# A third seven-product chunk per eight, with one weight sum formed by an accumulating load

## The chip, the cores and the metric

The kernel runs on one core of one Trainium2 chip. The metric is the device time of one execution in microseconds (us), as the median of several runs. In the text PE is TensorE, DVE is VectorE, ACT is ScalarE, POOL is GpSimd and SP is SyncE, as in the profile.

## The reference

One encoder layer on a sequence of 256 tokens of width 2048, in float32, and a final norm. What is computed:

```
x = x + 1/2 * SwiGLU_1(RMSNorm(x))        # w_gate, w_up: 2048 x 5632, w_down: 5632 x 2048
h = RMSNorm(x)
u, v, g = split(h @ w_in)                 # w_in: 2048 x 7168
x = x + (sigmoid(g_a) * PoolBranch(u) + sigmoid(g_b) * ConvBranch(v)) @ w_out
x = x + 1/2 * SwiGLU_2(RMSNorm(x))
out = RMSNorm(x)
SwiGLU(h) = (silu(h @ w_gate) * (h @ w_up)) @ w_down
```

Nearly all of the arithmetic is in the products with weights, and most of that in the two SwiGLU blocks (called FFN below). The change touches these two blocks alone; the part between them, called the mixer, stays as it is.

## The kernel before

**Precision.** Every product is formed from two-part operands: a number w is split into a high part `wh` (a cast on ACT) and a low part `wl` = w - wh (a subtraction on DVE), and x·w is xh·wh + xh·wl + xl·wh. So each block of a product costs three matmuls, and each weight that is loaded costs one ACT cast and one DVE subtraction (`hi_lo`).

**Units and chunks.** The weights come as a stream of chunks. A chunk is two rows of blocks, each a 128 x 1024 tile of 512 KB: `r0` holds blocks w11 (left half) and w12 (right half), `r1` holds w21 and w22. The tokens form two halves of 128 as well, so a chunk is a 2 x 2 by 2 x 2 block product. Normally this takes eight block products, 24 matmuls of 128x512. A unit is a run of chunks that adds into one set of accumulators in PSUM: a *gate unit* (512 hidden columns of gate and of up: 8 chunks, c0 to c7 below) or a *down unit* (1024 output columns; 8 chunks). An FFN has eleven gate units, numbered 0 to 10, and down units in pairs after gate units 4 and 8 and at the end. Gate unit 0 and the last pair take all products in the plain way; the ten other gate units and four down units of each FFN, 28 units in all, are *seven units*.

**Seven products.** In the chunks of a seven unit that `SEVEN` names (before: c0 and c3), a Strassen-Winograd form takes seven block products, 21 matmuls. It needs three sums of weight blocks, formed by four DVE additions (`split_seven`): S1 = w12 + w11, S1 + w22, w12 + w22 and S1 + w22 + w21. Three of them are split together (`exth`, `extl`, 128x1536), S1 takes w12's place in `r0`. It also needs four differences of the left operand, the *E forms* (`e_forms`: four DVE differences, an ACT cast, a DVE subtraction). For the gate products they are made once per FFN, for the down products whenever a hidden block is put in place. Four of the seven products go to PSUM banks 0 to 3 and are spread over the accumulators by `shared_parts` (one ACT copy, four DVE operations), the three others go straight to the accumulators in banks 4 to 7.

**Order.** Nothing is scheduled automatically: each engine executes its instructions in the order in which they are written, and waits where an operand is missing. `run` goes through the stream; at step i it issues the loads of chunk i+2, then the split of chunk i+1, then what stands in the table `side` for step i (`at`), then the products of chunk i. Work put into `middle` (`amid`) is written between the two halves of a plain chunk's matmuls. At the end of a gate unit (`gate_done_seven`) DVE adds the PSUM accumulators to the shared parts (two additions of 128x1024, one for each half of the tokens), ACT takes silu and DVE the product, giving the hidden tile h; the next unit's products into banks 4 to 7 wait for those two additions. h is transposed on PE one unit later by `put`, twice (k0 = 0 and 2): four transposes, an ACT cast, a DVE subtraction, and where the block belongs to a seven chunk an ACT copy `hy` and the E forms. The tiles `wh` and `wl` have four buffers each, two chunks' worth, so DVE and ACT run at most one chunk ahead of PE.

Of the kernel before, what the change touches and what calls it, by code (L numbers as in the profile page):

```python
# [8 lines left out]
F32 = mybir.dt.float32  # L9
# [29 lines left out]
TAPS_BUSY = 4  # L39

GROUP = 4
SEVEN = (0, 3)

B_P1, B_P5, B_P6, B_P7, B_11, B_12, B_21, B_22 = range(8)

# [36 lines left out]
def encoder_kernel(ctx: ExitStack, tc: tile.TileContext, x, xT, vecs, rows, pool_m,  # L82
# [30 lines left out]
    def at(i, fn):  # L113

        side.setdefault(i, []).append(fn)
# [19 lines left out]
    def raw_tile(name):  # L135
        return wraw.tile([P, W2], F32, tag="raw", name=name)

    def load(i):
        if i >= len(stream):
            return  # L140
        u, cc = stream[i]
        raw[i] = []
        for kk in range(2):
            r = raw_tile(f"raw{i}_{kk}")
            for c in range(0, W2, C if i == 0 else W2):
                s = slice(c, c + (C if i == 0 else W2))
# [3 lines left out]
            raw[i].append(r)  # L150

    def hi_lo(src, h, l=None):
        nc.scalar.copy(out=h, in_=src)  # L153
# [32 lines left out]

    def split_seven(i, r0, r1):

        w11, w12, w21, w22 = r0[:, :C], r0[:, C:], r1[:, :C], r1[:, C:]
        sm = ffn["pool"].tile([P, 3, C], F32, tag="sum", name=f"sum{i}")  # L190

        def add(out, a, b):
            nc.vector.tensor_tensor(out=out, in0=a, in1=b, op=ALU.add)  # L193
# [100 lines left out]

        return [tuple(block(pool, f"h{s}{u}", F32R, f"{name}{s}{u}") for s in "hl") for u in range(GROUP)]

    def e_tiles(pool, tag, n):

        return {c: tuple(pool.tile([P, 4, P], F32R, tag=f"{tag}E{x}{c}", name=f"{tag}E{x}{c}_{n}") for x in "hl")
                for c in SEVEN}  # L300

    def e_forms(dst, even, odd):

        e = stg.tile([P, 4, P], F32, tag="sg", name=f"e{Pos.now}")
        a11, a21, a12, a22 = even[:, :P], even[:, P:], odd[:, :P], odd[:, P:]
        for n, (a, b) in enumerate(((a11, a21), (a21, a22), (a11, e[:, 1, :]), (a12, e[:, 2, :]))):
            nc.vector.tensor_tensor(out=e[:, n, :], in0=a, in1=b, op=ALU.subtract)  # L307
        hi_lo(e, *dst)
# [8 lines left out]

    def scaled_forms(dst, src, gain_base, k0):

        y = stg.tile([P, 2, T], F32, tag="sg", name=f"y{Pos.now}_{k0}")  # L320
# [49 lines left out]
    def open_ffn(stack, n):  # L370

        pool = ffn["pool"] = stack.enter_context(tc.tile_pool(name=f"ffn{n}", bufs=1))
        ffn["ht"] = hidden(pool, f"ht{n}")
        ffn["hE"] = e_tiles(pool, "h", n)
        ffn["t0"], ffn["t1"] = (pool.tile([P, 2, C], F32, tag=f"part{t}", name=f"part{n}_{t}") for t in range(NT))

    def ffn_units(w_g, w_d, xt, xE, rs, residual_done, tail=None):
        waiting = []

        def hidden_lhs(k, t):  # L380
            return tuple(h[:, k % 4, t * P:(t + 1) * P] for h in ffn["ht"][k // 4])

        def put(u, hs, k0, b=None):
            b = transposes(lambda j, t: hs[t][:, (k0 + j) * P:(k0 + j + 1) * P], 2, f"hT{Pos.now}_{k0}", b)
            hi_lo(b.rearrange("p (q t) -> p q t", q=2), *(h[:, k0:k0 + 2, :] for h in ffn["ht"][u % GROUP]))
            c = (u % GROUP) * 2 + k0 // 2
            if c in SEVEN:
                y = stg.tile([P, 2, T], F32, tag="sg", name=f"hy{Pos.now}_{k0}")
                nc.scalar.copy(out=y, in_=b.rearrange("p (q t) -> p q t", q=2))
# [92 lines left out]
        for u in range(units):  # L482
            if u:
                add_unit(Unit(w_g[u], KD, lhs_of(xt), gate_done_seven(u), forms=forms_of(lhs_of(xt), xE),
                              early=gate_early, seven=SEVEN, start=(lambda: None) if u == 1 else None))
            else:
                add_unit(Unit(w_g[u], KD, lhs_of(xt), gate_done(u)))
# [13 lines left out]


    xt1 = pair(xtp, "x", KD, "xt1")
    xE1 = e_tiles(xtp, "x", 1)

    def start():
        nc.vector.memset(ones, 1.0)
# [11 lines left out]

    def load_x(t):  # L520
        nc.sync.dma_start(out=X[t], in_=x[t * P:(t + 1) * P, :])
        at(5, lambda: squares(t, 0, 0, D))
        if t == NT - 1:
            at(5, lambda: finish_rstd(rstd[0]))
# [12 lines left out]


    ht_stack = ExitStack()
    open_ffn(ht_stack, 1)  # L540
    xt2 = pair(xtp, "x", KD, "xt2")
    ffn_units(w_g1, w_d1, xt1, xE1, rstd[0], next_operand(xt2, V_NM, rstd[1]))
    n1 = len(stream)
# [263 lines left out]
    def wo_done(half):  # L807
        def done(acc):
            if half == 0:
                xt3.extend(pair(xtp, "x", KD, "xt3"))  # L810
                xE3.update(e_tiles(xtp, "x", 3))
# [65 lines left out]
    at(n3 - 1, final_first_half)  # L877


    xr = [block(ffn["pool"], f"xr{j}", F32, f"xr{j}") for j in range(4)]  # L880
    start()
    for i in range(PF - 1):
        load(i)
# [9 lines left out]
        at(2 + t, lambda t=t: load_x(t))  # L893
    at(KD // 2, lambda: nc.gpsimd.dma_start(out=vec[:, KD:], in_=vecs[:, KD:]))
    for c in SEVEN:
        at(c + 3, lambda c=c: scaled_forms(xE1[c], [xr[c // 2][:, 2 * c % 4 + j, :] for j in range(2)], V_N1, 2 * c))
    run(0, n1)
    ht_stack.close()

# [14 lines left out]

    ht_stack = ExitStack()
    open_ffn(ht_stack, 2)
    run(n2, n3)
    for i in sorted(side):
        for fn in side[i]:
# [88 lines left out]
```

## Time and profile before

| | |
|---|---|
| median of 3 runs | 1958.94 us (1958.81 to 1959.25) |
| the profiled execution | 1958.93 us, its span 1957.1 us |
| PE busy | 1933.4 us, 99% of the span |
| DVE busy | 1521.7 us, 78% (80 to 85% in most of the FFNs) |
| ACT busy | 979.2 us, 50% |
| POOL busy | 11.0 us |
| loads on SP's queue | 378.45 MB, 58.7% of the 16 DMA engines' time |
| granted PE clock | 0.998 |

The span of the profiled execution lies 1.8 us under its device time; that execution and the median agree. In a timeline row the first number is the start in us from the beginning of the span, the second the time in us from the start of the first instruction of the row to the end of the last; "x4" means that four instructions were merged. A bracket tells how long the engine sat idle before the row, and who ended that. A wait on another engine's result shows as idle time in front of the waiting instruction. Matmuls overlap, so their own duration (0.39 us) is longer than the distance from one to the next.

### The profile page before, as it was taken

To read this page: it belongs to the slowest core of one execution; us is meant where nothing else is said; L and a number is where in the kernel's file an instruction comes from. 1 tells how busy PE (TensorE), PEld (TensorE's weight loads), DVE (VectorE), ACT (ScalarE), POOL (GpSimd) and SP (SyncE) were. 2 spreads that over 40 slices of the span, in tenths; PEclk is the share of its full clock that TensorE was granted. 3 is DMA by queue.
4 is the path that set the end of the run, shared out by engine and by line. 5 is a ranking of instruction groups with operands and counts; after the bars stand their busy time and mean duration, and the time that the engine had idled before them with its cause. 6 is when DMAs were issued, how large, how long until landed. Compare 5 with 4: busy or idle time off the path is not lost.

```text
span 1957.1 us, 23246 instructions
## 1 busy us (share of the span) xinstructions
PE 1933.4 (99%) x8680; PEld 1598.3 (82%) x8680; DVE 1521.7 (78%) x1762; ACT 979.2 (50%) x1117; POOL 11.0 (1%) x22
## 2 busy tenths in 40 slices
PE   9999999999999999999999999999999999999998
PEld 7788888878888888888888887887888887888886
DVE  6888888888888655888898766588887888888865
ACT  6545544555445455454444545455554455455544
POOL 0000000000000000000000000000000000000000
PEclk9999999999999999999999999999999999999999
DMA  8555666555565556656666555555656565556654
GB/s 314 178 180 191 205 205 203 194 184 191 187 212 190 197 187 200 193 195 213 201 207 199 191 183 180 185 187 179 203 194 214 195 194 182 193 196 203 196 193 149
DMA packets 106145, 383.90 MB, mean 196 GB/s; under 512 B 11920, under 2 KB 12176, under 8 KB 105776
## 3 DMA queue, kind: packets, MB, share of 16 engines
q1 hardware_dynamic: 104688, 378.45, 58.7%
q0 software_dynamic: 1056, 3.83, 0.6%
q8 instruction: 68, 1.11, 0.2%
q14 instruction: 45, 0.37, 0.1%
q10 hardware_dynamic: 288, 0.14, 0.0%
HBM read 380.28 MB, written 2.10 MB: 195 GB/s over the span
## 4 chain that ended last, share of the span: by engine, by line
PE 94%; DVE 3%; ACT 1%; issue 1%; DMA 1%; DVEq 0%; POOLq 0%; ACTq 0%; POOL 0%
PE ps L256 78%; PE ps L277 13%; PE ps L343 1%; DVE wl L155 1%; DVE sum L193 1%; DVE part L413 0%; DVE extl L155 0%; ACT exth L153 0%; ACT wh L153 0%; DVE e L307 0%; DMA raw<-in_w_g 0%; PE ps L740 0%; ACT sq L358 0%; DMA xr<-in_xT 0%; PE ps L715 0%
## 5 line engine op out<-in xcount | busy, mean ns | idle before, releaser
L153 ACT CAST wh<-raw 128x1024 fp32r<-128x1024 f32 (+1 forms) x706 | 729.2, 1049 | 729.5 <-PE ps L256 361.6
L155 DVE TENSOR_TENSOR wl<-raw,wh 128x1024 fp32r<-128x1024 f32 (+1 forms) x706 | 846.2, 1219 | 316.4 <-ACT wh L153 312.8
L256 PE MATMUL ps<-wh,xt1h 128*128 128x512 f32 x544 | 169.9, 393 | 1.3 <-ACT wh L153 1.0
L256 PE MATMUL ps<-wh,xt3h 128*128 128x512 f32 x544 | 169.6, 393 | 0.0
L256 PE MATMUL ps<-wl,xt1h 128*128 128x512 f32 x544 | 168.3, 390 | 0.4 <-DVE wl L155 0.3
L256 PE MATMUL ps<-wl,xt3h 128*128 128x512 f32 x544 | 168.1, 390 | 0.3 <-DVE wl L155 0.3
L256 PE MATMUL ps<-wh,xt1l 128*128 128x512 f32 x544 | 167.7, 389 | 0.1
L256 PE MATMUL ps<-wh,xt3l 128*128 128x512 f32 x544 | 167.6, 389 | 0.0
L256 PE MATMUL ps<-wh,xt2h 128*128 128x512 f32 x448 | 138.5, 390 | 0.0
L256 PE MATMUL ps<-wh,xt2l 128*128 128x512 f32 x448 | 138.0, 389 | 0.0
L256 PE MATMUL ps<-wl,xt2h 128*128 128x512 f32 x448 | 137.9, 389 | 0.0
L256 PEld LDWEIGHTS ps<-wl,xt1h 128*128 128x128 f32 x544 | 101.9, 188 | 22.9 <-DVE wl L155 1.6
L256 PEld LDWEIGHTS ps<-wl,xt3h 128*128 128x128 f32 x544 | 101.9, 188 | 22.6 <-DVE wl L155 1.2
L256 PEld LDWEIGHTS ps<-wh,xt1l 128*128 128x128 f32 x544 | 102.0, 188 | 22.0 <-DVE xt1l L335 0.5
L256 PEld LDWEIGHTS ps<-wh,xt3l 128*128 128x128 f32 x544 | 102.1, 188 | 21.7
L256 PEld LDWEIGHTS ps<-wh,xt1h 128*128 128x128 f32 x544 | 100.5, 188 | 22.0 <-ACT wh L153 1.6
L256 PEld LDWEIGHTS ps<-wh,xt3h 128*128 128x128 f32 x544 | 100.5, 188 | 19.6
L155 DVE TENSOR_TENSOR extl<-sum,exth 128x1536 fp32r<-128x1536 f32 x56 | 98.5, 1759 | 22.9 <-ACT exth L153 22.9
L256 PEld LDWEIGHTS ps<-wl,xt2h 128*128 128x128 f32 x448 | 84.1, 188 | 17.6
L256 PEld LDWEIGHTS ps<-wh,xt2l 128*128 128x128 f32 x448 | 84.1, 188 | 17.5
L599 DVE SCALAR_TENSOR_TENSOR conv<-gluT,vec,conv 128x241 f32<-128x241 f32 (+14 forms) x240 | 97.0, 473 | 0.0
L256 PEld LDWEIGHTS ps<-wh,xt2h 128*128 128x128 f32 x448 | 83.3, 188 | 16.7
(237 smaller groups left out, 2852.6 us busy)
## 6 DMA issues: line engine op xcount, KB each, us to landing
raw<-in_w_g SPq DMA_DIRECT2D x350, 512.0 KB, 4.2
raw<-in_w_d SPq DMA_DIRECT2D x176, 512.0 KB, 4.0
raw<-in_w_in SPq DMA_DIRECT2D x112, 512.0 KB, 3.9
raw<-in_w_out SPq DMA_DIRECT2D x32, 512.0 KB, 4.2
raw<-in_w_pp SPq DMA_DIRECT2D x16, 512.0 KB, 3.8
raw<-in_w_cp SPq DMA_DIRECT2D x16, 512.0 KB, 3.6
row<-in_rows POOLq DMA_DIRECT2D x7, 512.0 KB, 4.0
X<-in_x SPq DMA_DIRECT2D x2, 1024.0 KB, 10.1
```

The source lines that it names most:

```text
L153: nc.scalar.copy(out=h, in_=src)
L155: nc.vector.tensor_tensor(out=l, in0=src, in1=h.bitcast(F32), op=ALU.subtract)
L193: nc.vector.tensor_tensor(out=out, in0=a, in1=b, op=ALU.add)
L256: nc.tensor.matmul(u.acc[t + c if u.tail and t else t][:, c, :], lhsT=a, rhs=b[:, c * C:(c + 1) * C], start=(t, c) not in u.begun, stop=k ...
L277: nc.tensor.matmul(ps[:, b, :], lhsT=x_, rhs=w_, start=where not in u.begun, stop=b < B_11 and cc == u.seven[-1] and n == 2)
L343: nc.tensor.transpose(out=b[:, j * T + t * P: j * T + (t + 1) * P], in_=src_of(j, t), identity=ident)
L599: nc.vector.scalar_tensor_tensor(out=dst, in0=src, scalar=w, in1=dst, op0=ALU.mult, op1=ALU.add)
```

## The change

`SEVEN` becomes c0, c2 and c4: three chunks of eight take 21 matmuls, 84 chunks in all instead of 56. The sums are made in another way. The right half of a seven chunk's `r0` is no longer loaded as w12. Step i loads w11 of chunk i+3 into the left half of a tile of its own (`load_left`, SP); one step later ACT copies the left half to the right, and POOL issues a load of w12 that adds into it (`add_right`), so that S1 stands there when the load has landed. DVE forms the other three sums in three operations instead of four. The copy and the accumulating load of chunk i+2 are written ahead of the split of chunk i+1.

Three pieces move. Both `put`s of a hidden tile, which stood ahead of two successive chunks (two and three steps after the last seven chunk), are now both in the middle of one chunk, two steps after the last seven chunk: c6. The E forms of a hidden block are written four steps later than its `put`, that is at c2 of the next unit. The E forms for the gate products are written one step later. The rest makes room (the hidden ring is opened later and shares tiles with the first operand; tiles get other pools) or is at the start of the kernel alone.

```diff
-SEVEN = (0, 3)
+SEVEN = (0, 2, 4)
...
@@ load
         for kk in range(2):
+            if kk == 0 and is_seven(i):
+                raw[i].append(summed.pop(i))
+                continue
...
+    def load_left(i):
+        if is_seven(i):
+            u, cc = stream[i]
+            summed[i] = ffn["pool"].tile([P, W2], F32, tag="r0", bufs=2, name=f"r0_{i}")
+            nc.sync.dma_start(out=summed[i][:, :C], in_=u.dram[u.k0 + 2 * cc, :, :C])
+
+    def add_right(i):
+        if is_seven(i):
+            u, cc = stream[i]
+            r = summed[i]
+            nc.scalar.copy(out=r[:, C:], in_=r[:, :C])
+            nc.gpsimd.dma_start(out=r[:, C:], in_=u.dram[u.k0 + 2 * cc, :, C:], accum_op=ALU.add)
...
@@ split_seven
-        w11, w12, w21, w22 = r0[:, :C], r0[:, C:], r1[:, :C], r1[:, C:]
+        w11, s1, w21, w22 = r0[:, :C], r0[:, C:], r1[:, :C], r1[:, C:]
...
-        add(sm[:, 1, :], w12, w22)
-        add(w12, w11, w12)
-        add(sm[:, 0, :], w12, w22)
-        add(sm[:, 2, :], sm[:, 0, :], w21)
+        for out, a, b, op in ((sm[:, 0, :], s1, w22, ALU.add), (sm[:, 1, :], sm[:, 0, :], w11, ALU.subtract),
+                              (sm[:, 2, :], sm[:, 0, :], w21, ALU.add)):
+            nc.vector.tensor_tensor(out=out, in0=a, in1=b, op=op)
...
@@ scaled_forms
-        e_forms(dst, y[:, 0, :], y[:, 1, :])
+        at(Pos.now + 1, lambda: e_forms(dst, y[:, 0, :], y[:, 1, :]))
...
@@ put
-                e_forms(ffn["hE"][c], y[:, 0, :], y[:, 1, :])
+                at(Pos.now + 4, lambda: e_forms(ffn["hE"][c], y[:, 0, :], y[:, 1, :]))
...
@@ gate_early
-                at(Pos.now + 1, lambda: put(u, hs, 0, ps[:, B_P6, :]))
-                at(Pos.now + 2, lambda: put(u, hs, 2, ps[:, B_P1, :]))
+                amid(Pos.now + 1, lambda: put(u, hs, 0, ps[:, B_P6, :]))
+                amid(Pos.now + 1, lambda: put(u, hs, 2, ps[:, B_P1, :]))
...
@@ run
             Pos.now = i
+            load_left(i + PF)
+            add_right(i + PF - 1)
             load(i + PF - 1)
             split_chunk(i + LEAD)
```

The rows below stand around the change from gate unit 2 (chunks 16 to 23) to gate unit 3 (24 to 31), or one unit later; `wl24_0` is the low part of chunk 24's first tile, `sum24` its weight sums, `extl24` their low part, `part` the accumulators of `gate_done_seven`, `h` the hidden tile, `ht` the transposed one, `e` and `hEl` the E forms.

DVE before, from the second `put` of unit 2 to the first plain split of unit 3:

```order
L155 TENSOR_TENSOR ht1l1_106<-ps_87,ht1h1_105 128x512
L307 TENSOR_TENSOR e22_1138<-hy22_2_1136 128x128 x2
...
L155 TENSOR_TENSOR hEl3_1_114<-e22_1138,hEh3_1_113 128x512
L193 TENSOR_TENSOR sum24_1173<-raw24_0_1118,raw24_1_1120 128x512
L193 TENSOR_TENSOR raw24_0_1118<-raw24_0_1118 128x512
...
L155 TENSOR_TENSOR extl24_1179<-sum24_1173,exth24_1178 128x1536
...
L413 TENSOR_TENSOR part1_0_115<-ps_87,part1_0_115 128x1024
...
L418 SCALAR_TENSOR_TENSOR h23_0_1218<-part1_0_115,rstd0_82 128x512
...
L155 TENSOR_TENSOR wl25_0_1227<-raw25_0_1169,wh25_0_1226 128x1024
...
L155 TENSOR_TENSOR wl26_0_1260<-raw26_0_1222,wh26_0_1259 128x1024
```

DVE now, from both `put`s of unit 2 to the third split of unit 3:

```order
L178 TENSOR_TENSOR ht0l1_577<-ps_87,ht0h1_576 128x512 x2
L216 TENSOR_TENSOR sum24_1202<-r0_24_1103,raw24_1_1148 128x512
...
L178 TENSOR_TENSOR extl24_1207<-sum24_1202,exth24_1206 128x1536
...
L435 TENSOR_TENSOR part1_0_111<-ps_87,part1_0_111 128x1024
...
L440 SCALAR_TENSOR_TENSOR h23_0_1246<-part1_0_111,rstd0_82 128x512
...
L178 TENSOR_TENSOR wl25_0_1255<-raw25_0_1198,wh25_0_1254 128x1024
...
L216 TENSOR_TENSOR sum26_1289<-r0_26_1196,raw26_1_1252 128x512
...
L178 TENSOR_TENSOR extl26_1294<-sum26_1289,exth26_1293 128x1536
...
L178 TENSOR_TENSOR wl27_0_1334<-raw27_0_1285,wh27_0_1333 128x1024
...
L326 TENSOR_TENSOR e26_1341<-hy22_0_1176 128x128 x2
...
L178 TENSOR_TENSOR hEl2_1_106<-e26_1341,hEh2_1_105 128x512
L216 TENSOR_TENSOR sum28_1373<-r0_28_1283,raw28_1_1331 128x512
```

The E forms went from ahead of `sum24` to ahead of `sum28`; the second seven chunk's sums (`sum26`) follow one plain split after the unit's end, where before two plain splits and c3 came.

ACT now, from the `put`s in gate unit 3 to the split of c2 of gate unit 4 (chunk 34):

```order
L176 CAST ht0h2_578<-ps_87 128x512
L411 COPY hy30_0_1519<-ps_87 128x512
L176 CAST ht0h2_578<-ps_87 128x512
L176 CAST wh32_0_1551<-r0_32_1446 128x1024
L176 CAST exth32_1549<-sum32_1545 128x1536
L176 CAST wh32_1_1557<-raw32_1_1491 128x1024
L436 ACTIVATE part1_0_111<-part1_0_111,rstd0_82 128x512
L436 ACTIVATE part1_1_112<-part1_1_112,rstd0_82 128x512
L172 COPY r0_34_1539<-r0_34_1539 128x512
L176 CAST wh33_0_1597<-raw33_0_1541 128x1024
L176 CAST wh33_1_1601<-raw33_1_1543 128x1024
L176 CAST wh34_0_1638<-r0_34_1539 128x1024
```

The copy for c2's accumulating load (`r0_34`) stands behind the two silus of the unit's end and ahead of c1's casts; before, c1's casts followed the silus at once.

More of the change, by code (lines that the diff above doesn't have):

```diff
@@ L150, in load, with is_seven @@
             raw[i].append(r)
+    def is_seven(i):
+        return i < len(stream) and isinstance(stream[i][0], Unit) and stream[i][1] in stream[i][0].seven
+    summed = {}
+    def load_left(i):
[9 more added lines that the diff above has]
+            nc.gpsimd.dma_start(out=r[:, C:], in_=u.dram[u.k0 + 2 * cc, :, C:], accum_op=ALU.add)
     def hi_lo(src, h, l=None):
@@ L378, in ffn_units, with open_hidden @@
         waiting = []
+        def open_hidden():
+            ffn["ht"] = hidden(ffn["pool"], f"ht{stream.index((first, 0))}")
         def hidden_lhs(k, t):
@@ L387, in put @@
             if c in SEVEN:
-                y = stg.tile([P, 2, T], F32, tag="sg", name=f"hy{Pos.now}_{k0}")
+                y = ffn["pool"].tile([P, 2, T], F32, tag="y", name=f"hy{Pos.now}_{k0}")
                 nc.scalar.copy(out=y, in_=b.rearrange("p (q t) -> p q t", q=2))
-                e_forms(ffn["hE"][c], y[:, 0, :], y[:, 1, :])
+                at(Pos.now + 4, lambda: e_forms(ffn["hE"][c], y[:, 0, :], y[:, 1, :]))
         def hidden_tile(t):
@@ L486, in ffn_units @@
             else:
-                add_unit(Unit(w_g[u], KD, lhs_of(xt), gate_done(u)))
+                first = Unit(w_g[u], KD, lhs_of(xt), gate_done(u))
+                add_unit(first)
+                at(len(stream), open_hidden)
             if u and u % GROUP == 0:
@@ L521, in load_x @@
         nc.sync.dma_start(out=X[t], in_=x[t * P:(t + 1) * P, :])
-        at(5, lambda: squares(t, 0, 0, D))
+        for half in range(2):
+            at(4 + t, lambda half=half: squares(t, 2 * half, half * W2, (half + 1) * W2))
         if t == NT - 1:
-            at(5, lambda: finish_rstd(rstd[0]))
+            at(6, lambda: finish_rstd(rstd[0]))
     def run(first, last):
@@ L877, in encoder_kernel @@
     at(n3 - 1, final_first_half)
-    xr = [block(ffn["pool"], f"xr{j}", F32, f"xr{j}") for j in range(4)]
+    xr = [block(ffn["pool"], f"h{x}{j}", F32, f"xr{x}{j}") for j in (2, 3) for x in "hl"]
     start()
@@ L895, in encoder_kernel @@
     for c in SEVEN:
-        at(c + 3, lambda c=c: scaled_forms(xE1[c], [xr[c // 2][:, 2 * c % 4 + j, :] for j in range(2)], V_N1, 2 * c))
+        at(c + 1, lambda c=c: scaled_forms(xE1[c], [xr[c // 2][:, 2 * c % 4 + j, :] for j in range(2)], V_N1, 2 * c))
     run(0, n1)
```

18 lines of the change are left out of this document (9 added, 9 removed).

## The prediction

> **What bounds the kernel now.** First the page's totals and its chain of waits.
>
> ```profile
> PE 1933.4 (99%) x8680; PEld 1598.3 (82%) x8680; DVE 1521.7 (78%) x1762; ACT 979.2 (50%) x1117; POOL 11.0 (1%) x22
> ...
> PE 94%; DVE 3%; ACT 1%; issue 1%; DMA 1%; DVEq 0%; POOLq 0%; ACTq 0%; POOL 0%
> ```
>
> PE sets the pace: 94% of the chain. So fewer matmuls are worth their time, as long as DVE delivers. The timeline of PE gives the distance between matmuls (their own 0.39 us overlap):
>
> ```profile
> 316.11 0.39 PE L277 MATMUL ps<-wh,xt1h 128*128 128x512 f32 x1
> ...
> 320.87 0.61 PE L256 MATMUL ps<-wh,xt1h 128*128 128x512 f32 x2
> ```
>
> One seven chunk lies between these rows: 21 matmuls in 4.76 us, 0.2267 each; a plain chunk of 24 takes 5.44.
>
> Then I read where DVE already shows on the chain. The chain in order of time, first FFN, rows that start at c1 of gate units 2, 3 and 4:
>
> ```profile
> 104.92 10.88 PE ps L256 x48
> ...
> 150.61 10.76 PE ps L256 x46
> ...
> 193.60 10.88 PE ps L256 x48
> ...
> 236.72 10.88 PE ps L256 x48
> ```
>
> 236.72 - 193.60 = 43.12 is the undisturbed period of a gate unit. The second row lacks its first two matmuls (0.45): c1 began at 150.16. The unit before it took 45.24 and the one after it 43.44: 2.4 us lost. What happened there, from the timelines of PE and DVE:
>
> ```profile
> 147.65 0.50 PE L277 MATMUL ps<-exth,xt1h 128*128 128x512 f32 x1 [1.66 <-DVE part L413]
> ...
> 150.61 0.74 PE L256 MATMUL ps<-wl,xt1h 128*128 128x512 f32 x2 [0.17 <-DVE wl L155]
> ```
>
> ```profile
> 134.24 0.68 DVE L155 TENSOR_TENSOR ht1l<-ps,ht1h 128x512 fp32r<-128x512 f32 x1
> 135.58 0.49 DVE L307 TENSOR_TENSOR e<-hy 128x128 f32<-128x128 f32 x2 [0.65 <-ACT hy L389]
> ...
> 137.41 0.69 DVE L155 TENSOR_TENSOR hEl<-e,hEh 128x512 fp32r<-128x512 f32 x1 [0.69 <-ACT hEh L153]
> 138.02 0.68 DVE L193 TENSOR_TENSOR sum<-raw,raw 128x512 f32<-128x512 f32 x1
> 138.74 0.69 DVE L193 TENSOR_TENSOR raw<-raw 128x512 f32<-128x512 f32 x1
> ...
> 140.19 0.69 DVE L193 TENSOR_TENSOR sum<-sum,raw 128x512 f32<-128x512 f32 x1
> 140.80 1.22 DVE L155 TENSOR_TENSOR wl<-raw,wh 128x1024 fp32r<-128x1024 f32 x1
> 142.44 1.76 DVE L155 TENSOR_TENSOR extl<-sum,exth 128x1536 fp32r<-128x1536 f32 x1 [0.41 <-ACT exth L153]
> 144.11 1.22 DVE L155 TENSOR_TENSOR wl<-raw,wh 128x1024 fp32r<-128x1024 f32 x1
> 145.25 2.35 DVE L413 TENSOR_TENSOR part<-ps,part 128x1024 f32<-128x1024 f32 x2
> ...
> 149.33 4.63 DVE L155 TENSOR_TENSOR wl<-raw,wh 128x1024 fp32r<-128x1024 f32 x4 [0.19 <-ACT wh L153]
> 153.99 0.69 DVE L193 TENSOR_TENSOR sum<-raw,raw 128x512 f32<-128x512 f32 x1
> ```
>
> DVE came late out of the `put` and the E forms, so both additions of the unit's end (145.25 to 147.60) held back c0's own products. The list of PE's waits (total, times, longest) shows how often:
>
> ```profile
> PE ps L277 <- DVE part L413: 6.6, 4, 1.7
> ```
>
> Four times: 4 x 2.4 = 9.6 us. Everywhere else DVE had room: two plain chunks follow before the next seven one.
>
> **The change, part by part.** *Matmuls.* The row of `extl` (one per seven chunk) counts
>
> ```profile
> L155 DVE TENSOR_TENSOR extl<-sum,exth 128x1536 fp32r<-128x1536 f32 x56 | 98.5, 1759 | 22.9 <-ACT exth L153 22.9
> ```
>
> 56 in 28 units; a third in each unit makes 28 more, with three matmuls less each: 84 x 0.2267 = 19.0 us off PE. The unit is then 5 x 5.44 + 3 x 4.76 + 0.8 for its eight transposes = 42.3 us.
>
> *The four old stalls* end, since the E forms leave that place: 9.6 us off. What takes their place is in the next term. With PE never waiting in the FFNs the profiled execution's 1958.9 would become 1930.3.
>
> *DVE's loop.* Now one loop per gate unit, from m, the middle of c6, where PE reaches the transposes. DVE stands there in order behind its waits; queued behind them are all of c0's split, the unit's end and the splits of c1 and c2. Durations, each from start to start in the rows above:
> - A split of a seven chunk was 138.02 to 145.25 = 7.23. Now the sums go 0.72 (dependent, as 138.02 to 138.74) + 0.61 + 0.61 (as 140.19 to 140.80); `extl` starts 2.25 after the last sum's start (140.19 to 142.44), is done 1.76 later, and the next split can start after 1.67 + 1.14: 6.39 in all, and `extl` is ready 5.34 after the first sum's start.
> - The `put`s. In the mixer ACT waits for eight such transposes (timelines of PE, of ACT there, and of ACT at the stall):
>
> ```profile
> 1152.41 1.03 PE L343 MATMUL ps<-ident,gate 128*128 128x128 f32 x8
> 1153.20 0.71 PE L256 MATMUL ps<-wh,mAh 128*128 128x512 f32 x2
> ```
>
> ```profile
> 1153.05 0.37 ACT L153 CAST mBh<-ps 128x256 fp32r<-128x256 f32 x1 [2.10 <-PE ps L343]
> ```
>
> ```profile
> 132.97 0.58 ACT L153 CAST ht1h<-ps 128x512 fp32r<-128x512 f32 x1
> 134.96 0.59 ACT L389 COPY hy<-ps 128x512 f32<-128x512 f32 x1 [1.41 <-DVE ht1l L155]
> ```
>
> Eight transposes 0.79; the cast 0.64 after the first; then cast 0.58, subtraction 0.68, `hy` 0.59 (it waits for the subtraction), second cast 0.58, second subtraction 0.61: DVE starts c0's sums 3.7 after m (2.5 without `hy`).
> - The unit's end: first addition 1.14 to the second's start. From there to c1's first `wl` 146.39 to 149.33 = 2.94, because c1's cast follows the second silu; the ACT copy now stands between them and adds 0.55 (a 128x512 piece takes ACT 0.58 in the rows above, the start of the next overlaps a little):
>
> ```profile
> 147.63 0.72 ACT L414 ACTIVATE part<-part,rstd 128x512 f32<-128x512 f32 x1 [0.41 <-DVE part L413]
> 148.26 3.88 ACT L153 CAST wh<-raw 128x1024 fp32r<-128x1024 f32 x4
> ```
>
> - Two plain `wl`: 149.33 to 153.99 holds four, so 2.3.
>
> Sum: c2's first sum starts at m + 3.7 + 6.4 + 1.1 + 3.5 + 2.3 = 17.0, its `extl` is ready at 22.4. PE, undisturbed, wants it at m + 0.8 + 2.7 + 5.4 (rest of c6, c7) + 4.8 + 5.4 (c0, c1) + 1.6 (six matmuls and one) = 20.7. DVE is 1.6 late. To c4's `extl` PE needs 10.2 more, DVE 6.4 + 2.3 + 2.44 for the E forms (135.58 to 138.02) = 11.1: another 0.9. From c4 PE leads back to m, so the delay isn't made up: **2.5 us per gate unit** that follows one with `hy`. These are gate units 2, 3, 4, 6, 7, 8 and 10, in two FFNs: 14 x 2.5 = 35.0. The down units after 4 and 8 follow a `put` without `hy` and have no E forms: 0.5 each (`extl` at 21.2), 2.0. Between down units there is no silu chain and no `put`; I put nothing there: DVE hides its adds of X in the 42 us unit, and would cost up to 1 us each, 8 us, if it didn't.
>
> *The accumulating load.* No row shows one. It starts when ACT's copy ends, at 1.24 (silu) + 0.63 + 0.58 = 2.45 after the second addition's start; DVE wants the sum at 3.5 + 2.3 = 5.8. So 3.3 us are hidden. Nearest rows, from issue to landing:
>
> ```profile
> row<-in_rows POOLq DMA_DIRECT2D x7, 512.0 KB, 4.0
> ...
> out_y<-X SPq DMA_DIRECT2D x8, 256.0 KB, 2.9
> ```
>
> ```profile
> DMA to landing us min/median/max: 3.7/4.0/5.2
> ```
>
> (the last row is the spread of `row`). The load reads 256 KB from memory and 256 KB of the tile, and writes 256 KB. Bounds: 2.9 and 5.2. I take 3.7, the fastest that 512 KB through POOL took, since only half is written: 0.4 beyond the cover in 18 places (the 14, and 4 down units that follow silus), 7.1 with 0.1 in the six other gate units. At 2.9: nothing. At 5.2: 1.9 x 18 + 1.6 x 6 = 43.
>
> The Trainium skill, DMA: Bandwidth & Descriptors, Anatomy of one DMA, fits a load from GpSimd as 2.0 us plus bytes over 436 GB/s. For 256 KB this is an estimate of 2.6 us, and the sum below would be 1967; for the row's 512 KB it gives 3.2, where the trace has 4.0, so the trace decides.
>
> Other terms are nothing: ACT gains 84 copies of 0.58 (50% busy, and their one tight place is counted); SP's left halves go out a chunk earlier than the copies need them, and if one were late ACT would hold c1's casts behind it; the 22 MB more that are read from tiles meet DMA engines at 58.7% (SP's queue, page). The edits at the start (E forms a step later, squares in halves) lie beside gate unit 0, whose chunks are all plain; with three sums fewer to make there, DVE covers them, and uncovered they would cost about 1 us.
>
> **Sum** on the profiled execution's clock, which is the median's: 1958.9 - 19.0 - 9.6 + 35.0 + 2.0 + 7.1 = **1974.4**.
>
> **Rivals.**
>
> *DVE keeps up (faster).* Its busy time speaks for it: per gate unit 3 x 6.4 + 5 x 2.3 + 2.3 + 1.6 + 2.6 + 1.3 + 2.4 = 41 of 42.3 us. Against it: the loop holds two waits (`put`, c1's cast) in which DVE can't work ahead. If the `put` chain and the silu chain were together 2.5 us shorter than I read, the 35 vanish and, with the load hidden, 1932 is left; with half of them 1950; 1941 in the middle.
>
> *The load is late (much slower).* POOL has little room: from a latency of 3.3 us on each us costs 18 to 24. At 5.2 us the sum is 1958.9 - 28.6 + 37 + 43 = 2010. For it: a read that must come back before the write. Against: the DMA engines are half idle.
>
> A rule bears on this: the Trainium skill, SBUF — State Buffer, Who interferes with whom, lets VectorE's two-port operations keep GpSimd from writing descriptors, but not tensor_tensor. Nearly all of DVE's rows here are TENSOR_TENSOR, so by that rule no delay; no run here shows one.
>
> *It cancels.* With a latency under 3.3 and 1.7 instead of 2.5 per unit (a `put` chain 0.8 shorter): 1958.9 - 28.6 + 23.8 + 2 = 1956. Nothing in the rows speaks for just this balance.
>
> **How the numbers follow.** Forecast, slower by DVE's loop (1962 to 1995): 0.50; late load (to 2012 and above): 0.15; DVE keeps up: 0.28; cancels: 0.07. A difference of 0.2% (4 us) is what a measurement of this kernel can tell. Faster 0.28, within 0.2% 0.08, slower 0.64. The range takes in most of the fast case and the late load at its bound: 1936 to 2011; the likeliest case's own is 1962 to 1995.
>
> **What would show it.** 8196 instead of 8280 matmuls of 128x512. In gate units 2 to 4: PE waiting at c0's own products for `part` (0.7 us), at c1's `wl` (about 1), at c4's `extl` (0.7 to 0.9); periods near 45 us instead of 43.1. `sum` rows that wait for a DMA under 0.5 us; more means the late load. If PE's periods are 42.3 and DVE shows no idle time after the silus, the loop was wrong, and so would I be if down units wait as well.

## The result and the profile after

The changed kernel takes 1988.11 us (median of 4 runs, 1986.84 to 1989.24); the kernel before took 1958.88 us beside it (4 runs, 1957.39 to 1959.25). The ratio is 1.0150, 95% interval 1.0133 to 1.0168: slower by 1.5%. The forecast was slower, 1974.4 us; the time lies inside both ranges, 14 us above the forecast. The profiled execution took 1987.74 us, its span 1986.0.

The page of the changed kernel, busy time of the engines and the chain of waits:

```profile
PE 1936.1 (97%) x8596; PEld 1575.8 (79%) x8596; DVE 1587.1 (80%) x1858; ACT 1063.2 (54%) x1247; POOL 84.7 (4%) x106
...
issue 53%; PE 41%; DVE 2%; DMA 2%; ACT 1%; POOL 0%; POOLq 0%; DVEq 0%; ACTq 0%; SPq 0%
```

PE has 84 instructions fewer and is busy 2.7 us longer: part of the time of a stop counts as busy (in the gate unit below PE is busy 43.80 us, in the run `best2` 42.37 with the same 192 instructions). The chain is of little use here ("issue" holds half of it, against 1% before), so the reading goes by PE's waits (engine, tile and line waited for; total us, times, longest):

```profile
PE ps L296 <- DVE extl L178: 16.3, 34, 1.3
PE ps L275 <- DVE wl L178: 8.7, 18, 0.5
PE ps L296 <- DVE part L435: 7.5, 14, 0.5
...
PE ps L296 <- DVE X L465: 1.3, 3, 0.6
```

`part` went from 4 waits to 14, each 0.5 instead of 1.7. In the list of before `extl` has one wait (1.3 us) and `wl` four of 0.2, so those two are all but new. One gate unit in the timeline, first PE from one unit's c0 to its c4, then DVE:

```profile
104.25 0.50 PE L296 MATMUL ps<-exth,xt1h 128*128 128x512 f32 x1 [0.54 <-DVE part L435]
107.72 0.73 PE L275 MATMUL ps<-wl,xt1h 128*128 128x512 f32 x2 [0.53 <-DVE wl L178]
114.94 0.50 PE L296 MATMUL ps<-extl,xEh 128*128 128x512 f32 x1 [0.34 <-DVE extl L178]
126.09 0.50 PE L296 MATMUL ps<-extl,xEh 128*128 128x512 f32 x1 [0.59 <-DVE extl L178]
```

```profile
95.48 0.68 DVE L216 TENSOR_TENSOR sum<-r,raw 128x512 f32<-128x512 f32 x1
...
101.85 2.35 DVE L435 TENSOR_TENSOR part<-ps,part 128x1024 f32<-128x1024 f32 x2
...
106.45 2.36 DVE L178 TENSOR_TENSOR wl<-raw,wh 128x1024 fp32r<-128x1024 f32 x2 [0.71 <-ACT wh L176]
109.47 0.69 DVE L216 TENSOR_TENSOR sum<-r,raw 128x512 f32<-128x512 f32 x1 [0.66 <-DMA r<-in_w_g]
...
113.12 1.76 DVE L178 TENSOR_TENSOR extl<-sum,exth 128x1536 fp32r<-128x1536 f32 x1 [0.50 <-ACT exth L176]
...
118.20 0.48 DVE L326 TENSOR_TENSOR e<-hy 128x128 f32<-128x128 f32 x2
...
120.64 0.68 DVE L216 TENSOR_TENSOR sum<-r,raw 128x512 f32<-128x512 f32 x1
...
124.28 1.76 DVE L178 TENSOR_TENSOR extl<-sum,exth 128x1536 fp32r<-128x1536 f32 x1 [0.49 <-ACT exth L176]
...
138.83 0.69 DVE L178 TENSOR_TENSOR ht0l<-ps,ht0h 128x512 fp32r<-128x512 f32 x1 [1.46 <-ACT ht0h L176]
140.66 0.69 DVE L178 TENSOR_TENSOR ht0l<-ps,ht0h 128x512 fp32r<-128x512 f32 x1 [1.14 <-ACT ht0h L176]
141.27 0.68 DVE L216 TENSOR_TENSOR sum<-r,raw 128x512 f32<-128x512 f32 x1
```

From first sum to first sum, 95.48 to 141.27, are 45.79 us. DVE waits at the `put`s (1.46 and 1.14), at c1's cast (0.71), at c2's load (0.66) and at the two `exth` shown. PE waits at the three places that the prediction listed (c0's own products, c1's `wl`, c4's `extl`), and also at c2's `extl`. The four listed waits are 2.0 us together.

The distance from one unit's first c0 matmul to the next one's, taken from PE's timeline of each kernel, gives the excess by kind of unit. "PE alone" is what the same unit takes in the run `best2` below, where PE waits for nothing there. The gate units are those of the first FFN; those of the second differ by 0.15 us at most.

| unit | before | after | PE alone |
|---|---|---|---|
| gate units 2, 3, 4 | 43.1, 45.6, 43.1 | 45.8, 45.8, 45.8 | 42.4 |
| gate units 6, 7, 8 | 43.1, 45.5, 43.1 | 45.7, 45.8, 45.9 | 42.4 |
| gate units 5 and 9 | 43.1 | 42.4 | 42.4 |
| down units, first of a pair | 42.16 | 42.6 to 43.4 | 41.48 |
| down units, second of a pair | 42.16 | 41.5 to 42.35 | 41.5 |

### The profile page after: what moved, and what is told of

Its sections match the earlier page's. It is cut to its first block, busy times and chain, and to the rows that moved or that the text cites. A ratio compares the mean times of both kernels' runs of the same rounds, so it can differ in the third digit from the quotient of the medians.

```text
span 1986.0 us, 23600 instructions
## 1 busy us (share of the span) xinstructions
PE 1936.1 (97%) x8596; PEld 1575.8 (79%) x8596; DVE 1587.1 (80%) x1858; ACT 1063.2 (54%) x1247; POOL 84.7 (4%) x106
## 4 chain that ended last, share of the span: by engine, by line
issue 53%; PE 41%; DVE 2%; DMA 2%; ACT 1%; POOL 0%; POOLq 0%; DVEq 0%; ACTq 0%; SPq 0%
PE ps L275 38%; PE ps L296 2%; PE ps L362 1%; DMA r<-in_w_d 1%; DVE sum L216 1%; DMA r<-in_w_g 1%; DVE wl L178 1%; DVE extl L178 0%; ACT exth L176 0%; DMA raw<-in_w_g 0%; POOL r L173 0%; ACT wh L176 0%; DVE X L465 0%; PE ps L768 0%; DMA xrh<-in_xT 0%
## 5 line engine op out<-in xcount | busy, mean ns | idle before, releaser
L178 DVE TENSOR_TENSOR wl<-raw,wh 128x1024 fp32r<-128x1024 f32 (+1 forms) x622 | 738.7, 1217 | 199.1 <-ACT wh L176 195.7
L176 ACT CAST wh<-raw 128x1024 fp32r<-128x1024 f32 (+1 forms) x622 | 635.7, 1047 | 366.6 <-PE ps L275 237.4
L176 ACT CAST exth<-sum 128x1536 fp32r<-128x1536 f32 x84 | 124.6, 1484 | 128.0 <-DVE sum L216 128.0
L178 DVE TENSOR_TENSOR extl<-sum,exth 128x1536 fp32r<-128x1536 f32 x84 | 147.7, 1758 | 39.1 <-ACT exth L176 39.1
L176 ACT CAST wh<-r 128x1024 fp32r<-128x1024 f32 x84 | 88.6, 1054 | 112.8 <-DMA r<-in_w_g 56.7
L275 PE MATMUL ps<-wh,xt1h 128*128 128x512 f32 x464 | 145.2, 394 | 2.6 <-ACT xt1h L353 1.6
L275 PE MATMUL ps<-wh,xt3h 128*128 128x512 f32 x464 | 144.8, 393 | 0.0
L275 PE MATMUL ps<-wh,xt1l 128*128 128x512 f32 x464 | 143.1, 389 | 0.0
L275 PE MATMUL ps<-wh,xt3l 128*128 128x512 f32 x464 | 142.9, 389 | 0.0
L178 DVE TENSOR_TENSOR wl<-r,wh 128x1024 fp32r<-128x1024 f32 x84 | 102.3, 1218 | 0.0
```

Of the source, the lines that this page charges most:

```text
L178: nc.vector.tensor_tensor(out=l, in0=src, in1=h.bitcast(F32), op=ALU.subtract)
L275: nc.tensor.matmul(u.acc[t + c if u.tail and t else t][:, c, :], lhsT=a, rhs=b[:, c * C:(c + 1) * C], start=(t, c) not in u.begun, stop=k ...
```

## The experiments

Gate units are named as in the prediction. The kernels of one group ran beside each other and share their runs of the kernel before (1958.8 to 1959.3 us).

### Without the accumulating load, and three moves in the order

`no_accum`:

```diff
             nc.scalar.copy(out=r[:, C:], in_=r[:, :C])
-            nc.gpsimd.dma_start(out=r[:, C:], in_=u.dram[u.k0 + 2 * cc, :, C:], accum_op=ALU.add)
```

> The changed kernel without the accumulating load: ACT still copies w11, but nothing is added to it, so the first sum is w11 + w22 instead of w11 + w12 + w22 (the output is that of other weights; the work of PE, DVE and ACT is unchanged). Theory 1 (DVE's loop through the put, the splits and the E forms, the load a small part): the list of VectorE's waits for r in the sums (15.9 us) vanishes, some of the stretch moves to the wait for the right halves of the next chunk; 1970 to 1977 us, and gate units still take about 45. Theory 2 (the accumulating load is what holds the kernel): gate units near 42.5, 1950 us or less. Theory 3 (VectorE's total work sets the pace): 1985 to 1988, since its work is the same.

Measured: 1967.47 us (1966.68 to 1968.01), 2.5 us under theory 1's range; 20.6 us less than with the load. One gate unit, as busy us of each engine between two first matmuls of c0 (the stretch and its length; then PE, PEld, DVE, ACT, POOL, the clock, the DMA engines' share and GB/s), with the load and without:

```profile
100.83:146.62 45.79, 43.80 (x192) 34.71 (x191) 38.79 (x44) 25.82 (x29) 2.60 (x3) 1.00 0.59 184
```

```profile
98.65:143.63 44.98, 43.45 (x192) 34.87 (x191) 38.70 (x44) 25.71 (x29) 0.00 (x0) 1.00 0.51 170
```

45.0 instead of 45.8, and the down units at 42.06 and 41.5. So most of a gate unit's excess, 45.0 - 42.4 = 2.6 us, is there without the load: theory 1. Theory 3 falls, since DVE's work is the same. But the load costs 21 us, not the 7 of the prediction. By unit: about 14 x 0.79 = 11.1 in the gate units, 5.9 in the down units, 3.0 at the starts of the two FFNs.

`e_late`, `put_start` and `e_late_put`, the last one with both edits:

```diff
-                at(Pos.now + 4, lambda: e_forms(ffn["hE"][c], ...))
+                at(Pos.now + (7 if u < 2 * GROUP else 4), lambda: e_forms(ffn["hE"][c], ...))
```

```diff
-                amid(Pos.now + 1, lambda: put(u, hs, 0, ps[:, B_P6, :]))
-                amid(Pos.now + 1, lambda: put(u, hs, 2, ps[:, B_P1, :]))
+                at(Pos.now + 1, lambda: put(u, hs, 0, ps[:, B_P6, :]))
+                at(Pos.now + 1, lambda: put(u, hs, 2, ps[:, B_P1, :]))
```

> The changed kernel with one number altered: the E forms of the hidden tiles (2.44 us of VectorE between the puts' ends and the next c4 of a gate unit) are made three chunks later, beside c5, where VectorE is past the loop; VectorE's total work is the same. Theory 1 (a chain of VectorE work per unit): the unit gets 2.0 to 2.4 us shorter in 12 units, 43.4 to 43.8 us, 1958 to 1964 us in all. Theory 2 (late load): 1980 to 1988, since the load's lateness stays. Theory 3 (total work): 1985 to 1990.

> The changed kernel with both transposes (the puts) issued at the start of c6 instead of in its middle, 2.7 us earlier on PE; no work is added or removed. Theory 1: the loop starts 2.2 to 2.7 us earlier, as long as VectorE has its E forms and splits for c6 and c7 done by then, gate units of 43.2 to 43.7, 1954 to 1962 us. Theory 2 (late load): the load starts as much earlier as the sums do, so 1985 to 1988. Theory 3 (total work): 1985 to 1990.

> Both moves together: E forms three chunks later and the puts at the start of c6. Theory 1: the loop would be 45.8 - 2.4 - 2.5 = 40.9, under PE's own 42.3, so PE sets the pace again: 1932 to 1942 us, with the load's lateness of 0.7 us now inside the slack; the down units after a put remain. Theory 2: about 1975 to 1988, the load still in the path. Theory 3: 1985 to 1990.

Measured: `e_late` 1979.46 (1977.94 to 1981.84), gate units 44.8 to 45.3; `put_start` 1968.48 (1967.78 to 1971.73), 44.2 to 45.3; both together 1970.88 (1970.67 to 1971.60), 43.5 to 45.7. Each helps alone. `e_late`, only 0.5 us under theory 2's range, would not decide it; `put_start`, 17 us under the ranges of theories 2 and 3, does: neither holds. But `e_late` gains 9 us where theory 1 expected 24 to 30, `put_start` 20 where it expected 26 to 34, and together, where it expected 1932 to 1942, they are no better than `put_start` alone.

The expectations were wrong because they took the whole length of a moved piece off the unit. The prediction's own loop gives less: DVE was to be 1.6 us late at c2 and another 0.9 at c4. E forms that are taken from between c2 and c4 can save only the 0.9 (measured 0.5 to 1.0 in a unit), and earlier `put`s only the 1.6, since the 0.9 stays (measured 0.5 to 1.7, on average 1.25). PE's timeline bears this out stretch by stretch (table in the section on the prediction): in `e_late` PE loses nothing from c4 on, and no less than before up to c2; in `put_start` it loses 1.2 us less up to c2, and as much as before from c4 on. And the E forms found no free place at c5. In `e_late_put`, the transposes of a `put` on PE, the casts of c6 and of the `put` on ACT, and DVE (`e` are the moved E forms):

```profile
176.86 1.09 PE L362 MATMUL ps<-ident,h 128*128 128x128 f32 x8
```

```profile
171.46 1.05 ACT L176 CAST wh<-raw 128x1024 fp32r<-128x1024 f32 x1 [2.34 <-PE ps L296]
...
178.28 0.59 ACT L176 CAST ht0h<-ps 128x512 fp32r<-128x512 f32 x1
```

```profile
172.54 1.22 DVE L178 TENSOR_TENSOR wl<-raw,wh 128x1024 fp32r<-128x1024 f32 x1 [1.07 <-ACT wh L176]
173.69 0.48 DVE L326 TENSOR_TENSOR e<-hy 128x128 f32<-128x128 f32 x2
...
176.12 2.00 DVE L454 TENSOR_TENSOR part<-ps,part 128x512 f32<-128x512 f32 x3
...
178.76 2.35 DVE L178 TENSOR_TENSOR wl<-raw,wh 128x1024 fp32r<-128x1024 f32 x2
181.03 0.68 DVE L178 TENSOR_TENSOR ht0l<-ps,ht0h 128x512 fp32r<-128x512 f32 x1
```

The `put`'s cast is done at 178.87 and DVE takes it up at 181.03, 2.2 us late, with no idle time ahead: 173.69 to 176.12 went to the E forms. DVE could not do them sooner, for before them it waits 1.07 us for c6's cast, and that cast has waited 2.34 us for PE's last products of c4, whose split tiles it needs (four buffers, one chunk ahead). So the loop has a second start: from the end of c4 on PE, through c6's split, the shared parts, c7's split, and only then the `put`. That start had been hidden behind the later one, m, by the 1.46 us for which DVE waits at `ht0l` in the changed kernel.

### The load a chunk earlier, four sums, and better orders

The theory was restated: the unit is DVE's work plus the short waits in its queue, in one loop, and a wait taken out of the queue is worth its length. `early_copy`:

```diff
-            ... tag="r0", bufs=2 ...
+            ... tag="r0", bufs=3 ...
@@ run
-            load_left(i + PF)
-            add_right(i + PF - 1)
+            load_left(i + PF + 1)
+            add_right(i + PF)
```

> The changed kernel with ACT's copy of w11 and the accumulating load behind it issued one chunk earlier (the left half's load too, and a third buffer for it). The first four runs made a theory: a gate unit of 45.8 us is 39.4 us of VectorE's work and some 6 us of its short waits, all in one loop; a wait that is taken from its queue is worth its length, and work that is moved is worth nothing unless it fills such a wait. Theory 1: the wait of c2's first sum for the load (0.66) goes, and the copy (0.55) no longer stands between the second silu and c1's cast, on which VectorE waits; units of 44.5 to 44.7, in all 1964 to 1971 us. Theory 2 (the load is late wherever it stands, since the DMA queues or the left half hold it): 1983 to 1988.

Measured: 1958.86 us (1957.73 to 1960.78), as long as the kernel before (ratio 1.000, 0.9991 to 1.0009) and 5 us under theory 1's range: its units of 44.5 are there, and the down units went to 41.5 as well. In DVE's timeline from c1's split to c2's first sum both waits are nearly gone (0.71 to 0.18, 0.66 to none):

```profile
148.61 2.36 DVE L178 TENSOR_TENSOR wl<-raw,wh 128x1024 fp32r<-128x1024 f32 x2 [0.18 <-ACT wh L176]
150.89 0.68 DVE L216 TENSOR_TENSOR sum<-r,raw 128x512 f32<-128x512 f32 x1
```

And that although the load itself has become slower. The rows of the accumulating load, time to landing (min, median, max), in the changed kernel with DVE's wait for it (us, times), and in `early_copy`, where DVE does not appear among those who waited for it:

```profile
  DVE sum L216: 15.9, 23
...
DMA to landing us min/median/max: 3.6/3.8/9.0
```

```profile
DMA to landing us min/median/max: 3.6/7.1/8.8
```

Of the 29.3 us that this move saves, 20.6 are what `no_accum` saves; the other 8.6 are put down to the copy, which no longer stands between the second silu and c1's cast (PE's wait for `wl` fell from 8.7 us to 1.0, and what PE loses up to c2 of a gate unit from 1.81 to 1.30). No run moved the copy without the load.

`four_sums` loads w12 in the plain way and makes all four sums on DVE, as the kernel before does, in three chunks:

```diff
-            load_left(i + PF)
-            add_right(i + PF - 1)
...
+        add(sm[:, 1, :], w12, w22)
+        add(w12, w11, w12)
+        add(sm[:, 0, :], w12, w22)
+        add(sm[:, 2, :], sm[:, 0, :], w21)
```

> Seven products in three chunks, but all four sums on VectorE from a plain load of w12 (no copy, no accumulating load). Theory 1 (VectorE's work and waits): each of the three splits 0.84 us longer (7.23 against 6.39), the load's wait (0.66 to 0.8) and the copy (0.55) gone: units of 46.9 to 47.2, 1998 to 2008 us. Theory 2 (the accumulating load is what costs): 1955 to 1970, as with the load left out.

Measured: 2008.54 us (2008.21 to 2008.83), 0.5 us above theory 1's range, units of 47.05. That is 44.5 (no load to wait for, no copy in the way) plus 3 x 0.84 = 2.5 for the longer splits: DVE's time in this loop adds up one to one. Theory 2 is out by 39 us. So the accumulating load as the change has it beats a fourth sum on DVE by 20 us; issued a chunk earlier, by 50.

`early_put` joins `early_copy` with the earlier `put`s; `early_put_pool` also moves the four small subtractions of the hidden E forms to GpSimd:

```diff
-            nc.vector.tensor_tensor(out=e[:, n, :], in0=a, in1=b, op=ALU.subtract)
-        hi_lo(e, *dst)
+            (eng or nc.vector).tensor_tensor(out=e[:, n, :], in0=a, in1=b, op=ALU.subtract)
+        if eng:
+            at(Pos.now + 2, lambda: hi_lo(e, *dst))
+        else:
+            hi_lo(e, *dst)
@@ put
-                at(Pos.now + 4, lambda: e_forms(ffn["hE"][c], ...))
+                at(Pos.now + 2, lambda: e_forms(ffn["hE"][c], ..., nc.gpsimd))
```

> The early copy and load together with the puts at the start of c6. Theory 1: 44.3 with the early puts alone, less the waits for the load (0.7 and 0.26 in a unit) and the copy's 0.55: 42.8 to 43.2 a unit, close to PE's 42.3; 1942 to 1952 us, faster than the kernel before. Theory 2: not under 1965, since something else of VectorE's loop (the wait for split buffers after c4, the put) takes the place of the waits.

> The same with the four small subtractions of the hidden E forms on GpSimd instead of VectorE, and their split two chunks later, so that nobody waits for GpSimd. Theory 1 (VectorE's work is the rest of the excess): 1.1 us of work and 0.7 of waiting leave its queue, units at PE's 42.3; 1934 to 1944 us. Theory 2 (GpSimd and VectorE disturb each other at the tiles' memory): VectorE's rows get longer while GpSimd works, and the time is 1945 us or more.

Measured: 1939.67 (1938.62 to 1940.96) and 1937.41 (1936.73 to 1938.51), ratios 0.9901 (0.9886 to 0.9916) and 0.9888 (0.9871 to 0.9904) to the kernel before. `early_put`, 2 us under theory 1's range, does the very work of the changed kernel, on the same engines, in another order (with a third buffer for `r0`), and is 48 us faster. The move to GpSimd gives little, 2 us: the time is in theory 1's range, but the units stay at 43.1 to 43.2 instead of 42.3, and DVE's rows get longer, as theory 2 had it (last section).

### Two seven chunks again, the copy `hy`, and all together

`two_seven` keeps every other edit of the change and takes the third seven chunk back (the `put`s, which stand two steps behind the last seven chunk, are then at c5); `two_seven_early` does the same on top of `early_copy`:

```diff
-SEVEN = (0, 2, 4)
+SEVEN = (0, 3)
```

> Every other edit of the change kept, but chunks 0 and 3 alone take seven products, as in the kernel before. Theory 1 (the third seven chunk closes VectorE's loop; the old four stalls went with the later E forms): two plain chunks stand between the sevens again, no stall of 2.4 us at the unit's end, gate units of 43.1 throughout: 1958.9 less up to 9.6, 1948 to 1953 us. Theory 2 (the copy, the accumulating load or the later E forms cost by themselves): 1957 us or more.

> Seven products in chunks 0 and 3 alone, with the copy and the accumulating load one chunk earlier. With the copy at its place this kernel kept 0.9 us of PE's waiting in a gate unit, beside waits of VectorE's sums for the load (80 us in all, up to 4.7 us each). Theory 1 (the load is what is left there): the sums no longer wait, the units take 43.1, and the time is the kernel before's less its four stalls: 1947 to 1952 us. Theory 2 (the copies on ACT, the later E forms or the third sum's order cost the 0.9): 1955 to 1959.

Measured: `two_seven` 1957.11 us (1954.58 to 1958.68), ratio 0.9988 (0.9978 to 0.9997): at the lower end of theory 2's range. The old stalls of 2.4 us are gone, but most gate units take 43.8 to 44.3 where they took 43.1. DVE's wait for the accumulating load (us, times), and its time to landing:

```profile
  DVE sum L216: 80.2, 46
...
DMA to landing us min/median/max: 3.7/6.4/7.7
```

With two chunks in the loop DVE comes to the sums sooner and the load later: 80 us of waiting against 16. Issued a chunk earlier (`two_seven_early`), the gate units take 43.05 throughout, and the time is 1941.67 us (1941.39 to 1941.92), ratio 0.9911 (0.9894 to 0.9927). So what `two_seven` lost was the load (with its copy, which moved too), as theory 1 of the second run had it; the time is 5 us below its range, because the start (the first seven unit begins at 51.8 instead of 53.1 us and takes 43.6 instead of 46.9) is faster too.

`hy_last` moves ACT's copy `hy` behind the second cast of the `put`s; `best2` has that, the early copy and load, the early `put`s, and the E forms on GpSimd:

```diff
                 y = ffn["pool"].tile([P, 2, T], F32, tag="y", ...)
-                nc.scalar.copy(out=y, in_=b.rearrange("p (q t) -> p q t", q=2))
+                kept.append((b, y))
...
+            if kept and (k0 or last_first):
+                b, y = kept.pop()
+                nc.scalar.copy(out=y, in_=b.rearrange("p (q t) -> p q t", q=2))
```

> The changed kernel with ACT's copy hy behind both casts of the puts instead of between them, so that the second cast does not wait for the first subtraction: 1.14 us of VectorE's waiting leave the loop in the units with hy, no work is added or removed. Theory 1 (work plus waits in one loop): units of 44.6 to 44.8 instead of 45.8, 1972 to 1977 us. Theory 2 (the start of the loop is PE's transposes and the rest has slack, so that the sums wait for the load instead): 1982 to 1988.

> The early copy and load, the early puts, the E forms on GpSimd, and hy behind both casts. Theory 1: the units of 43.15 lose what PE still waits at c0's own products and at c1 (0.3 and 0.3), and reach 42.4 to 42.6: 1928 to 1934 us. Theory 2: what is left in these units is not VectorE's, and the time stays at 1936 to 1939.

Measured: `hy_last` 1972.87 us (1970.69 to 1974.82), as theory 1 had it, most units at 44.5 to 44.7: the 1.14 us of the second `ht0l` row were worth 1.1 in the unit. `best2` 1926.84 us (1925.50 to 1927.17), ratio 0.9834 (0.9819 to 0.9848), 1 us under theory 1's range. Its gate units take 42.37; one of them as busy us (columns as above), and the chain of the page:

```profile
98.61:140.98 42.37, 42.37 (x192) 35.19 (x191) 38.88 (x40) 25.62 (x29) 7.21 (x7) 1.00 0.62 199
```

```profile
PE 98%; ACT 1%; DVE 1%; issue 0%; DMA 0%; DVEq 0%; POOLq 0%; POOL 0%; ACTq 0%
```

PE sets the pace again. DVE is busy 38.88 us in this unit and 38.79 in that of the changed kernel, which takes 3.4 us more: what the change ran into was not too much work on DVE, but about 3.5 us of waits in its queue that lay in the loop. With them out, the third seven chunk is worth about 1941.67 - 1926.84 = 14.8 us (its matmuls 19.0; less 1.2 before the first seven unit and 2.0 in it, and about 1 elsewhere). `best2` has three edits more than `two_seven_early` (the earlier `put`s, `hy`, the E forms on GpSimd), but the gate units of both are at PE's own time, 42.37 and 42.37 + 0.68 = 43.05, so these edits have nothing left to gain there.

## Why the prediction was right, and where it was off

*The matmuls, -19.0.* PE counts 84 fewer, and a down unit that waits for nothing went from 42.16 to 41.48: 0.68 is three matmuls at 0.2267. Right.

*The four stalls, -9.6.* Right as a term: in `two_seven_early` the units of 45.5 take 43.05. That "their place" would be taken by the next term was right as well.

*DVE's loop, +35.0.* Without the load (`no_accum`) a unit takes 45.0, 2.6 over 42.38; 14 x 2.62 = 37, where 2.5 each had been forecast. PE waits at the three places listed; units 5 and 9, which follow a down unit and no `put`, stay at 42.4; and the `put` chain was 3.7 (the transposes start at 137.58 in the changed kernel, the sums at 141.27). What the prediction missed is that this loop has a second start close behind the first (`e_late_put`). It changes nothing in the sum, but everything in what a repair is worth.

```profile
137.58 1.03 PE L362 MATMUL ps<-ident,h 128*128 128x128 f32 x8
```

What PE loses in a gate unit against `best2`, by stretch (mean of gate units 2, 3, 4, 6, 7 and 8 of both FFNs, from the starts of c0, c2, c4 and the next unit's c0 in PE's timelines), shows the sizes:

| us lost by PE | c0 to c2 | c2 to c4 | from c4 on |
|---|---|---|---|
| prediction, without the load | 1.6 (DVE's lateness at c2's `extl`) | | 0.9 |
| `no_accum` | 1.81 | 0.00 | 0.81 |
| the changed kernel | 1.81 | 0.67 | 0.95 |
| `e_late` | 2.05 | 0.66 | 0.00 |
| `put_start` | 0.57 | 0.65 | 0.96 |
| `early_copy` | 1.30 | 0.00 | 0.85 |
| `early_put` | 0.16 | 0.00 | 0.74 |
| `early_put_pool` | 0.80 | 0.00 | 0.00 |

PE's wait at c2's `extl` comes with the load: in `no_accum` it is gone, and in PE's timeline of the same unit the three others stand:

```profile
102.07 0.50 PE L295 MATMUL ps<-exth,xt1h 128*128 128x512 f32 x1 [0.54 <-DVE part L434]
105.55 0.73 PE L274 MATMUL ps<-wl,xt1h 128*128 128x512 f32 x2 [0.53 <-DVE wl L177]
123.11 0.50 PE L295 MATMUL ps<-extl,xEh 128*128 128x512 f32 x1 [0.47 <-DVE extl L177]
```

*The down units, +2.0.* First of a pair in `no_accum`: 42.06 against 41.48, four times 0.58. Right. That nothing would happen between them: right without the load.

*The accumulating load, +7.1: the step that failed, by its size.* It costs 20.6. All the other terms give 1974.4 - 7.1 = 1967.3, and `no_accum` takes 1967.5; that they meet so closely is in part luck, since the loop and the down units came out 2.0 us above their terms and the starts of the FFNs somewhat below. (The term itself is loosely rounded: 18 x 0.4 + 6 x 0.1 is 7.8.) Of the 20.6, 11.1 are in the 14 gate units, where 14 x 0.4 = 5.6 stood. The price of 3.7 us was right there: in all twelve units read, c2's first sum starts 3.68 to 3.85 us after POOL issues the load. But the sum let the load start when ACT's copy ends. In the unit shown the copy ends at 105.47, and POOL issues the load at 105.76 (the bracket names `h`, but the distance from the copy's end is 0.28 to 0.33 us in 83 of the 84 loads, whatever the bracket names):

```profile
104.86 0.61 ACT L172 COPY r<-r 128x512 f32<-128x512 f32 x1
```

```profile
105.76 0.87 POOL L173 DMA_DIRECT2D r<-in_w_g  x1 [20.09 <-DVE h L440]
```

These 0.29 us were put at nothing. So DVE waits 0.66 instead of 0.4, and PE loses 0.67 at c2 and 0.14 more from c4 on.

In the down units (5.9 where 4 x 0.4 = 1.6 stood) some loads took twice the price: four of them 7.1 to 8.7 us from issue to use. (The 3.0 at the starts of the FFNs were not followed up.) In the changed kernel, the issue of the load for a down unit's c0 on POOL, and the sum that waited for it on DVE:

```profile
267.02 0.87 POOL L173 DMA_DIRECT2D r<-in_w_d  x1 [15.27 <-DVE wl L178]
```

```profile
274.31 0.70 DVE L216 TENSOR_TENSOR sum<-r,raw 128x512 f32<-128x512 f32 x1 [0.75 <-DMA r<-in_w_d]
```

7.3 us from issue to use, beyond the upper bound of 5.2, which had been taken from seven loads of the mixer. A single latency for 84 loads, bounded by rows from another stage, was the second error; in `two_seven` and `early_copy` the median itself is 6.4 and 7.1.

*The rivals.* "DVE keeps up" did not come true, though an order in which it does exists (`early_put`, `best2`). The late load had a right mechanism and a third of the excess (20.6 of the 61 us between the changed kernel and `best2`), but not its 2010 us. The estimate of 2.6 us from the Trainium skill (DMA: Bandwidth & Descriptors, Anatomy of one DMA) was too low: in no run here did an accumulating load land in under 3.6 us.

## What to carry to other kernels

When an engine off the bound feeds it in a ring of few buffers, write its queue out as a loop with its starts (each place where it must wait for the bound engine), and price a repair by how late it is at each place where it hands over, not by the length of what is moved: the next start or the next late place takes the rest. A load on such a path is to be priced at the latency that it has beside the other loads, and the repair is to issue it earlier, not to make it faster. Before a change is dropped because the helper engine looks full, compare its busy time per unit with the unit: 38.8 of 45.8 us became 38.6 of 43.2 by order alone (`early_put`, mean of two units), and 38.9 of 42.4 in `best2`, where four small subtractions also went to GpSimd.

## What the runs showed of the hardware that was not expected

**The accumulating load's latency depends on when it is issued.** The same 256 KB took 3.8 us (median) in the changed kernel, 6.4 in `two_seven`, 7.1 in `early_copy`, but 4.6 in `two_seven_early`. In `two_seven` DVE waited until 109.83 for the load that POOL issued at 102.69, and SP issued four raw loads of 512 KB from 102.22 on. That these delayed it fits, but no run varied them alone, so the cause stays open.

**Between ACT's copy and the issue of the load on POOL lie 0.3 us.** In the changed kernel POOL's issue starts 0.28 to 0.33 us after the end of the copy in 83 of the 84 loads.

**A stop of PE costs more than its listed wait.** In a unit of the changed kernel the four waits listed add up to 2.0 us, while the unit is 45.79 - 42.37 = 3.42 longer than one without waits: some 0.35 more at each stop. PE's rows around the stop at c4 tell where it goes:

```profile
125.10 0.40 PE L296 MATMUL ps<-exth,xEh 128*128 128x512 f32 x1
126.09 0.50 PE L296 MATMUL ps<-extl,xEh 128*128 128x512 f32 x1 [0.59 <-DVE extl L178]
126.42 0.40 PE L296 MATMUL ps<-exth,xEl 128*128 128x512 f32 x1
```

From one start to the next are 0.99 us instead of 0.2267, so 0.76 are lost, 0.17 more than the listed 0.59: the list counts idle time from the end of a matmul that normally overlaps with the next. The matmul behind the stop then comes after 0.33 us, and the next ones stay a little slow as well; that makes up the rest. Why they are slow is not shown (the granted clock in this unit is 1.00).

**GpSimd's subtractions slowed VectorE's.** In `best2` the rows of both while GpSimd forms `e`, POOL first:

```profile
134.32 1.72 POOL L326 TENSOR_TENSOR e<-hy 128x128 f32<-128x128 f32 x2
136.12 3.27 POOL L326 TENSOR_TENSOR e<-hy,e 128x128 f32<-128x128 f32 x2
```

```profile
133.56 0.69 DVE L216 TENSOR_TENSOR sum<-sum,r 128x512 f32<-128x512 f32 x1
134.17 1.58 DVE L216 TENSOR_TENSOR sum<-sum,raw 128x512 f32<-128x512 f32 x1
135.68 1.46 DVE L178 TENSOR_TENSOR wl<-r,wh 128x1024 fp32r<-128x1024 f32 x1
```

A sum of 0.68 takes 1.58, a `wl` of 1.22 takes 1.46. That is why DVE's busy time per unit did not fall (38.83 in `early_put_pool`, 38.79 in the changed kernel) although four of its instructions had left. PE's loss from c4 on goes (0.74 to 0.00 us in a unit), but slower sums make it lose 0.80 instead of 0.16 up to c2, and the gain is 2 us. The Trainium skill, SBUF — State Buffer, Who interferes with whom, has a VectorE instruction with two inputs in SBUF contend with a GpSimd instruction that reads SBUF; these rows agree.
